# Three edits to the mixers and the first attention: GpSimd's long operations on VectorE, selection rows on 128 rows, logits made kind by kind

## The chip, the cores and the metric

The kernel runs on one core of a Trainium2 chip. The metric is the device time of one execution in microseconds (us). PE is TensorE, which multiplies matrices; DVE is VectorE, ACT is ScalarE, POOL is GpSimd, and SP is SyncE, whose queue issues the loads of weights. Each engine works through its own queue in order, and waits there on semaphores for the others.

## The reference, cut to what matters

There are 256 tokens of width 1024 and three blocks of layers: a first block with a gated recurrence (HGRN2), a forgetting attention and a hierarchical mixture of experts; then twice a SwiGLU, a mixer of three kinds, and a second SwiGLU. The change touches the attention's logits and the mixers.

```python
def fox_mixer(...):                       # 8 heads of 64; blocks of 128 queries
    logits = einsum('bhtd,bhsd->bhts', qb, k) + (cb[..., :, None] - cum[..., None, :])
    logits = where(mask, logits, NEG_INF)
    p = softmax(logits)
...
def ssd_chunked(x, dt, a, bm, cm):        # 16 heads of 64, run forwards and backwards
    seg = a_cs[:, :, :, None] - a_cs[:, :, None, :]
    decay = exp(where(lower, seg, -inf))
    cb = einsum('bclgn,bcsgn->bclsg', cc, bc)
    y_diag = einsum('bclsg,bclsgr,bcsgrp->bclgrp', cb, decay, xd)
...
def second_block(...):                    # for l in range(2)
    y_ssd = ssd_mixer(...); y_mla = mla_mixer(...); y_conv = conv_mixer(...)
    x = x + concatenate([y_ssd, y_mla, y_conv]) @ w_out[l]
```

## The kernel before, in words

**Products.** Every product with weights is done three times in fp32r (`mm3`, L296 to L299): high part by high part, high by low, low by high. `load` (L257 to L280) brings a tile of weights in by SP's queue as `raw`, ACT casts it to `hi` (L275), and one engine subtracts (`lo` = `raw` − `hi`, L276). `hi` and `lo` have five buffers each, and SP's next load waits for the subtraction that frees its `raw`. The subtraction is DVE's unless the caller names another engine.

**Order.** The phases run one after another: first block, mixture of experts, then for each of two layers SwiGLU, mixer, SwiGLU. A scheduler sets the order in every engine's queue from the order of the program, with loads given priority. PSUM has four banks for running work (`wk`) and four for sums (`acc`).

**The first attention's logits** (L772 to L785). Six units make a bank each: four units of two heads by 256 keys, two of four heads by 128 keys. For each head three matmuls go into its part of the bank: q by k with the 64 rows of a head (L781), a row of cumulative decays chosen by a selection matrix on 128 rows (L782), and the causal mask (L783).

**The mixer.** Three kinds of sequence layer make 28 tiles of 128 columns; each is multiplied by its rows of `w_out` and summed. The convolution's group norm takes its inverse roots as a row tile `cvrow`, spread to columns by `epair` (L1405 to L1437), and gives `yn` and its parts `oh` and `ol`. The state-space layer (SSD) works through pairs of heads i = 0 to 7 (loop L1639 to L1653). `decay(i)` (L1549 to L1571), for each of two directions d, puts a mask (L1554) and differences of cumulative decays (L1558, L1562) into a bank; these come from rows chosen by `esel`, held on 48 partitions. ACT takes the exponential (L1564), DVE adds the two (L1567) and multiplies by `cb` (L1569): this is `m`. `outputs(i)` (L1573 to L1606) spreads a row by `epair` (L1576, 48 rows), multiplies `cb` with `xu` (L1584) and `m` with `xt` (L1589, 64 columns), and DVE makes `v` and `y` (L1591 to L1595). Then come `xh` on ACT and `xl` on DVE (L1598, L1599) and the sum of squares `ssq` (L1605). `project(i)` (L1608 to L1624) multiplies by `w_out`. `project_others` (L1626 to L1636) does so for the attention and the convolution while the scan runs.

**GpSimd's share.** Before the change POOL makes, in each of the two mixers, 16 subtractions L276 of `w_out` (the loads in `project` and `project_others`), four `xu` products (L1534) and four of six sums L1605. It also does the convolutions' tap sums (L1368, L1393) and small roots (L307), which stay.

**DVE's chain.** The latent attention's output norm puts a chain of some 15 small operations on DVE: L1840, L305, then Newton's steps of an inverse root in L316 to L321, then L1843. In its queue it lies between `m` of one pair of heads and `y` (L1591, L1593) of the next; `add_to_X` (L331, L333) adds sums to the residual `X`.

Of the kernel before, what the change touches and what calls it, by code (L numbers as in the profile page):

```python
# [11 lines left out]
F32R = mybir.dt.float32r  # L12
# [3 lines left out]
OP = mybir.AluOpType  # L16
# [3 lines left out]
P = 128  # L20
T = 256
# [186 lines left out]
class Kern:  # L208
# [553 lines left out]
    def fox_steps(self, mp, fq, fk, fv, cum, o):  # L762


        nc = self.nc
        e, hd = self.fox_e, self.fox_head
        units = [(1, 0, 0), (1, 1, 0), (1, 0, 2), (1, 1, 2), (0, 0, 0), (0, 1, 0)]
        st = {}

        def heads(u):  # L770
            t, par, j0 = units[u]
            return t, (t + 1) * P, [par + 2 * (j0 + j) for j in range(4 - 2 * t)]  # L772

        def logits(u):
            t, n, hs = heads(u)
            if u == 0:
                st["nh"] = self.split_rows(0, 8, cum[2], -1.0)
            ps = self.bank()
            for j, h in enumerate(hs):
                r = ps[:, j * n:(j + 1) * n]  # L780
                nc.tensor.matmul(r, hd(fq, h)[:, t * P:(t + 1) * P], hd(fk, h)[:, :n], start=True, stop=False)  # L781
                nc.tensor.matmul(r, e(h, P), st["nh"][:, :n], start=False, stop=False)  # L782
                nc.tensor.matmul(r[:, n - P:], self.identb, self.maskb[1], start=False, stop=True)  # L783
            p = st["p", u] = self.t512(mp, "p")
            self.softmax(mp, p, ps, len(hs), 1.0)  # L785

        def turn(u):
            p = st.pop(("p", u))
            ps = self.bank()
            for i in range(4):  # L790
                s = slice(i * P, (i + 1) * P)
                nc.tensor.transpose(ps[:, s], p[:, s], self.ident)
            pt = st["t", u] = self.t512(mp, "pt")
            self.evacuate(pt, ps, u % 2)

        def values(u):
            t, n, hs = heads(u)
            pt = st.pop(("t", u))
            ps = self.bank()
            nb = t + 1  # L800
            for j, h in enumerate(hs):
                for s in range(nb):
                    i = j * nb + s
                    nc.tensor.matmul(ps[:, j * 96:(j + 1) * 96], pt[:, i * P:(i + 1) * P],
                                     fv[:, s, h * 65:h * 65 + 96], start=s == 0, stop=s == nb - 1)
            pair = o[:, t].rearrange("p (a two) d -> p a two d", two=2)
            _, par, j0 = units[u]
            self.normalise_heads(mp, pair[:, j0:j0 + len(hs), par], ps, len(hs))

        return logits, turn, values  # L810


# [390 lines left out]
    def mix_tables(self):  # L1203

        nc = self.nc
        c = self.ctx.enter_context(self.tc.tile_pool(name="late", bufs=1))
        self.epair = c.tile([48, 16, 64], F32R, name="epair")
        nc.vector.tensor_copy(self.epair, self.cfs("esel")[:48].unsqueeze(2).to_broadcast([48, 16, 64]))
        self.rows48 += [self.zero_row(c, i) for i in range(1, 5)]
        posi = c.tile([P, TB], I32, name="posi")  # L1210
        nc.scalar.dma_start(posi, self.io["pos"])
        posf = c.tile([P, TB], F32, name="posf")
        nc.vector.tensor_copy(posf, posi)
        ang = c.tile([P, 2, TB, 16], F32, name="ang")
        kk = c.tile([P, 2, TB, 16], F32, name="angk")
        for t in range(TB):
            nc.vector.tensor_scalar(ang[:, 1, t], self.cfs("inv"), posf[:, t:t + 1], None, op0=OP.mult)
        nc.vector.tensor_scalar(kk[:, 1], ang[:, 1], 1.0 / (2 * math.pi), None, op0=OP.mult)
        nc.vector.tensor_scalar(kk[:, 0], kk[:, 1], 0.25, None, op0=OP.add)
        nc.vector.tensor_copy(ang[:, 0], ang[:, 1])  # L1220
        big = 12582912.0
        nc.vector.tensor_scalar(kk, kk, big, None, op0=OP.add)
        nc.vector.tensor_scalar(kk, kk, -big, None, op0=OP.add)
        c1 = 6.28125
        c2 = float((np.asarray(2 * math.pi - c1, np.float32).view(np.uint32) & np.uint32(0xFFFFF000)).view(np.float32))
        c3 = float(np.float32(2 * math.pi - c1 - c2))
        for cc in (c1, c2, c3):
            nc.vector.scalar_tensor_tensor(ang, kk, -cc, ang, op0=OP.mult, op1=OP.add)
        nc.vector.tensor_scalar(ang[:, 0], ang[:, 0], math.pi / 2, None, op0=OP.add)
        lim = 3.1415925  # L1230
        nc.vector.tensor_scalar(ang, ang, lim, -lim, op0=OP.min, op1=OP.max)
        self.cs = c.tile([P, 2, TB, 32], F32, name="cs")
        for h in range(2):
            nc.scalar.activation(self.cs[:, :, :, 16 * h:16 * h + 16], ang, AF.Sin)
# [169 lines left out]
    def conv_rms(self, mp, cv):  # L1404

        nc = self.nc
        sel = self.cfs("half8").rearrange("p (i a) -> p i a", i=4)
        ps = self.bank()
        for c in range(2):
            sq = self.t512(mp, "cvsq").rearrange("p (a t) -> p a t", a=2)  # L1410
            nc.scalar.activation(sq, cv["y"][:, 2 * c:2 * c + 2], AF.Square)
            for j in range(2):
                i = 2 * c + j
                nc.tensor.matmul(ps[:8, :T], sel[:, i], sq[:, j], start=i == 0, stop=i == 3)
        z = mp.tile([48, T], F32R, name="cvrow", tag="xp0")
        nc.vector.tensor_scalar(z, self.ones[:48].to_broadcast([48, T]), 0.0, None, op0=OP.mult)
        r = mp.tile([8, T], F32, name="cvr", tag="xp1")
        nc.vector.tensor_tensor(r, ps[:8, :T], cv["invb2"][:8], op=OP.mult)
        nc.vector.tensor_scalar(r, r, 1.0 / 64, EPS, op0=OP.mult, op1=OP.add)
        self.newton(r, r, self.t256(mp, "cvr1")[:8], self.t256(mp, "cvr2")[:8])  # L1420
        nc.vector.tensor_tensor(r, r, cv["invb"][:8], op=OP.mult)
        nc.scalar.copy(z[:8], r)
        nc.vector.tensor_tensor(z[32:40], r, z[:8].bitcast(F32), op=OP.subtract)
        cv["row"] = z
# [88 lines left out]
    def ssd_operands(self, mp, S, xs):  # L1513

        nc = self.nc
        u = S["u"]
        xt = mp.tile([P, TB, 16, 64], F32, name="xt", tag="qT")
# [3 lines left out]
        def group(g):  # L1521
            ps = self.bank()
# [6 lines left out]
            for t in range(TB):  # L1529
                ps = self.bank()  # L1530
                for i in range(4):
                    nc.tensor.transpose(ps[:, i * P:(i + 1) * P], xs[:, 4 * g + i, t * P:(t + 1) * P], self.ident)
                nc.scalar.copy(xt[:, t, 8 * g:8 * g + 8].rearrange("p h q -> p (h q)"), ps)
                nc.gpsimd.tensor_tensor(xu[:, t, 8 * g:8 * g + 8], xt[:, t, 8 * g:8 * g + 8],  # L1534
                                        u[:, 16 * t + 8 * g:16 * t + 8 * g + 8].unsqueeze(2).to_broadcast([P, 8, 64]),
                                        op=OP.mult)
        S["xt"], S["xu"], S["cb"] = xt, xu, cb
# [2 lines left out]
    def ssd_scan(self, l, mp, S, xs, zs, wout, mla, cv):  # L1540
# [6 lines left out]
        def decay(i):  # L1547

            ms = []  # L1549
            for d in range(2):  # L1550
# [3 lines left out]
                nc.tensor.matmul(gp, self.identb, self.maskb[d].unsqueeze(1).to_broadcast([P, 4, P]),  # L1554
                                 start=True, stop=False)
                for j in range(2):
                    e = self.esel[:48, 2 * i + j:2 * i + j + 1].to_broadcast([48, P])
                    nc.tensor.matmul(gv[:, j], e, tgt[:48], start=False, stop=False)  # L1558
                e = self.esel[:48, 2 * i:2 * i + 2].unsqueeze(2).to_broadcast([48, 2, P])
                for t in range(TB):  # L1560
                    ts = slice(t * P, (t + 1) * P)
                    nc.tensor.matmul(gv[:, :, ts], src[:48, ts], e, start=False, stop=t == 1)  # L1562
                m = self.t512(mp, f"m{d}")
                nc.scalar.activation(m, gp, AF.Exp)  # L1564
                ms.append(m)
# [7 lines left out]
        def outputs(i, mv):  # L1573
            g = i // 4
            vp = self.bank()
            nc.tensor.matmul(vp[:, :T], self.epair[:, 2 * i:2 * i + 2].rearrange("p a q -> p (a q)"), S["tx"][:48],  # L1576
                             start=True, stop=True)
            v = self.t256(mp, "v")
            nc.scalar.activation(v, vp[:, :T], AF.Exp)
# [20 lines left out]
            if i % 4 == 0:  # L1600
                nc.scalar.activation(ssq[:, g], y, AF.Square)
            else:
                sq = self.t256(mp, "sq")
                nc.scalar.activation(sq, y, AF.Square)
                (nc.vector if i % 4 == 3 else nc.gpsimd).tensor_tensor(ssq[:, g], sq, ssq[:, g], op=OP.add)  # L1605
            return hh, hl  # L1606

        def project(i, hh, hl):  # L1608
# [1 line left out]
            if i % 4 == 0:  # L1610
                S["acc"] = [[self.bank("acc") for _ in range(2)] for _ in range(TB)]
            if i % 2 == 0:
                S["wt"] = self.load(wout[2 + i // 2], eng=nc.gpsimd)
            if i % 4 < 3:
                self.out_tile(S["acc"], S["wt"], i % 2, hh, hl, i % 4 == 0, False)
                return
# [7 lines left out]
                          lambda n, t: self.add_to_X(t, n, S["acc"][t][n], inv[:, g, t:t + 1]))  # L1624

        def project_others(c, ops, n, tag):  # L1626
            wt = self.load(wout[c + n], eng=nc.gpsimd)
            for t in range(TB):
                ps = self.bank(tag)
                if c and n == 1 and t == 1:  # L1630
# [282 lines left out]
```

## Time and profile before

| | us |
|---|---|
| median of 3 runs (lowest to highest) | 1656.97 (1656.61 to 1661.03) |
| the profiled execution | 1659.93 |
| its span on the engines | 1658.1 |
| PE busy | 1605.6 (97%) |
| DVE busy | 1031.5 (62%) |
| ACT busy | 747.2 (45%) |
| POOL busy | 166.3 (10%) |

In the chain that ended last PE holds 62% and DVE 9% of the span. A share over the whole span says little here, since the stages differ. The two scans of the state-space layer lie at about 754 to 840 us and 1374 to 1460 us, the first attention at about 65 to 110 us, and the mixture of experts from about 148 to 410 us. A row of the timeline has the start, the time of the group, engine, line, what is written and read, and partitions x columns; in brackets stands the engine's idle time before it and what ended that.

### The profile page before, as it was taken

The page shows a single profiled execution, that of the slowest core. Times are in us where ns is not written, and L with a number is a line of the kernel's source. Part 1 is how long each engine was busy: PE and PEld are TensorE (multiplying, and loading weights), DVE is VectorE, ACT ScalarE, POOL GpSimd, SP SyncE. Part 2 cuts the span into 40 slices and gives each one's busy share as a digit, 9 for nine tenths or more (in the row PEclk, how much of TensorE's full clock was granted, in tenths as well). Part 3 has the DMA queues.
Part 4 walks back from the last instruction along what each step waited for, and adds up shares of the span by engine and source line. Part 5 has one row for each costly group of instructions (what it writes and reads, how often), then busy time and mean ns, then how long its engine had stood idle before and what let it go on. Part 6 is the DMA issues. An engine that isn't in the chain of part 4 may idle for free.

```text
span 1658.1 us, 25503 instructions
## 1 busy us (share of the span) xinstructions
PE 1605.6 (97%) x10407; PEld 1344.7 (81%) x10407; DVE 1031.5 (62%) x1645; ACT 747.2 (45%) x1219; POOL 166.3 (10%) x145
## 2 busy tenths in 40 slices
PE   8999899997999999998999999999999998999999
PEld 7987444433999989996789998999989996799998
DVE  6967221112756579887765566656569887766564
ACT  5544111111644467554464444444467554454443
POOL 0320000000000002115400000000001115400000
PEclk9999999999999999999999999999999998999999
DMA  9323899998755234432245555455544432245552
GB/s 381 136 77 133 330 415 417 417 417 352 288 187 187 72 136 165 153 106 99 76 153 204 178 182 187 165 180 191 174 167 153 153 120 84 77 156 200 178 193 87
DMA packets 50958, 320.37 MB, mean 193 GB/s; under 512 B 5904, under 2 KB 6160, under 8 KB 17680
## 3 DMA queue, kind: packets, MB, share of 16 engines
q1 hardware_dynamic: 50256, 318.04, 51.9%
q8 instruction: 84, 1.38, 0.3%
q10 hardware_dynamic: 576, 0.60, 0.1%
q14 instruction: 42, 0.34, 0.1%
HBM read 317.58 MB, written 1.05 MB: 192 GB/s over the span
## 4 chain that ended last, share of the span: by engine, by line
PE 62%; DVE 9%; ACT 2%; issue 2%; POOL 0%; ACTq 0%; DVEq 0%
PE wk L297 10%; PE wk L298 10%; PE wk L299 10%; PE acc L297 9%; PE acc L299 9%; PE acc L298 9%; DVE lo L276 2%; DVE xs L1370 1%; ACT hi L275 1%; PE wk L1793 1%; PE wk L1774 1%; DVE ol L1436 1%; PE wk L1558 0%; DVE m L1567 0%; DVE q L1741 0%
## 5 line engine op out<-in xcount | busy, mean ns | idle before, releaser
L276 DVE TENSOR_TENSOR lo<-raw,hi 128x1024 fp32r<-128x1024 f32 (+2 forms) x312 | 378.4, 1224 | 203.1 <-ACT hi L275 199.0
L275 ACT CAST hi<-raw 128x1024 fp32r<-128x1024 f32 (+1 forms) x344 | 354.7, 1042 | 329.3 <-PE wk L298 125.6
L297 PE MATMUL wk<-xh,hi 128*128 128x256 f32 x1344 | 380.7, 283 | 0.0
L299 PE MATMUL wk<-xh,lo 128*128 128x256 f32 x1344 | 380.1, 283 | 0.0
L298 PE MATMUL wk<-xl,hi 128*128 128x256 f32 x1344 | 380.0, 283 | 0.0
L298 PEld LDWEIGHTS wk<-xl,hi 128*128 128x128 f32 x1344 | 257.5, 192 | 1.9
L297 PEld LDWEIGHTS wk<-xh,hi 128*128 128x128 f32 x1344 | 257.5, 192 | 1.7
L299 PEld LDWEIGHTS wk<-xh,lo 128*128 128x128 f32 x1344 | 257.6, 192 | 0.0
L297 PE MATMUL acc<-xh,hi 128*128 128x256 f32 x688 | 199.5, 291 | 0.2
L299 PE MATMUL acc<-xh,lo 128*128 128x256 f32 x688 | 194.7, 283 | 1.8 <-DVE lo L276 1.8
L298 PE MATMUL acc<-xl,hi 128*128 128x256 f32 x688 | 194.7, 283 | 0.5 <-DVE xl L372 0.5
L297 PE MATMUL acc<-hi,hh 128*128 128x512 f32 x352 | 139.5, 397 | 0.4 <-ACT hh L447 0.3
L298 PE MATMUL acc<-lo,hh 128*128 128x512 f32 x352 | 138.6, 395 | 0.0
L299 PE MATMUL acc<-hi,hl 128*128 128x512 f32 x352 | 137.4, 396 | 0.0
L297 PEld LDWEIGHTS acc<-xh,hi 128*128 128x128 f32 x688 | 131.0, 191 | 3.1 <-issue 1.3
L299 PEld LDWEIGHTS acc<-xh,lo 128*128 128x128 f32 x688 | 131.4, 191 | 2.4 <-DVE lo L276 2.2
L298 PEld LDWEIGHTS acc<-xl,hi 128*128 128x128 f32 x688 | 131.6, 191 | 1.9 <-DVE xl L372 0.9
L276 DVE TENSOR_TENSOR lo<-more,hi 128x1024 fp32r<-128x1024 f32 x64 | 81.1, 1276 | 33.2 <-ACT hi L275 32.8
L275 ACT CAST hi<-more 128x1024 fp32r<-128x1024 f32 x64 | 66.0, 1044 | 48.1 <-PE wk L298 18.4
L436 DVE TENSOR_TENSOR gu<-wk,invb 128x512 f32<-128x512 f32 x84 | 58.0, 691 | 47.3 <-PE wk L299 47.2
L276 POOL TENSOR_TENSOR lo<-raw,hi 128x1024 fp32r<-128x1024 f32 x32 | 76.6, 2398 | 94.2 <-ACT hi L275 94.2
L447 ACT CAST hh<-h 128x256 fp32r<-128x256 f32 x88 | 35.7, 406 | 101.9 <-DVE h L444 101.8
(450 smaller groups left out, 2564.7 us busy)
## 6 DMA issues: line engine op xcount, KB each, us to landing
raw<-in_ffn_dram SPq DMA_DIRECT2D x112, 1024.0 KB, 4.7
more<-in_wmoe_dram SPq DMA_DIRECT2D x39, 1024.0 KB, 15.0
raw<-in_win_dram SPq DMA_DIRECT2D x37, 1024.0 KB, 4.8
whole<-in_wmoe_dram SPq DMA_DIRECT2D x66, 512.0 KB, 12.6
raw<-in_wmoe_dram SPq DMA_DIRECT2D x24, 1024.0 KB, 12.7
more<-in_ffn_dram SPq DMA_DIRECT2D x20, 1024.0 KB, 4.8
raw<-in_wout_dram SPq DMA_DIRECT2D x17, 1024.0 KB, 4.9
more<-in_win_dram SPq DMA_DIRECT2D x7, 1024.0 KB, 13.6
```

Source lines behind the costliest of these rows:

```text
L275: nc.scalar.copy(hi[:, :sub], raw[:, s])
L276: (eng or nc.vector).tensor_tensor(lo[:, :sub], raw[:, s], hi[:, :sub].bitcast(F32), op=OP.subtract)
L297: nc.tensor.matmul(out, ah, bh, start=start, stop=False)
L298: nc.tensor.matmul(out, ah, bl, start=False, stop=False)
L299: nc.tensor.matmul(out, al, bh, start=False, stop=stop)
L436: nc.vector.tensor_tensor(gu, gate.rearrange("p (a t) -> p a t", a=2), invb.unsqueeze(1).to_broadcast([P, 2, T]), op=OP.mult)
L447: nc.scalar.copy(hh, h)
L1370: nc.vector.scalar_tensor_tensor(o, xp[:, j, q:q + T], cwh[:, 12 * q + i:12 * q + i + 1], o, op0=OP.mult, op1=OP.add)
L1436: nc.vector.tensor_sub(hl, yn, hh.bitcast(F32))
L1774: nc.tensor.matmul(ps[:, j * T:(j + 1) * T], qT[:, h + j, t * P:(t + 1) * P], kT[:, h + j], start=True, stop=True)
L1793: nc.tensor.matmul(ps[:, j * 96:(j + 1) * 96], pt[:, i * P:(i + 1) * P], v[:, s, (h + j) * 65:(h + j) * 65 + 96], start=s == 0, stop=s == 1)
```

## The change

1. Logits: per unit, first all L782 (128 rows), then one mask matmul over all heads of the unit in place of one each, then all q by k (64 rows).
2. `epair` and `cvrow` grow from 48 to 128 partitions, and L1558, L1562, L1576 read 128 rows in place of 48; the added rows hold zeros.
3. The subtractions for `w_out`, the products `xu` and all sums `ssq` are DVE's: 16 + 4 + 4 operations in each mixer.

```diff
-            for j, h in enumerate(hs):
-                r = ps[:, j * n:(j + 1) * n]
-                nc.tensor.matmul(r, hd(fq, h)[:, t * P:(t + 1) * P], hd(fk, h)[:, :n], start=True, stop=False)
-                nc.tensor.matmul(r, e(h, P), st["nh"][:, :n], start=False, stop=False)
-                nc.tensor.matmul(r[:, n - P:], self.identb, self.maskb[1], start=False, stop=True)
+            rs = [ps[:, j * n:(j + 1) * n] for j in range(len(hs))]
+            m = len(hs)
+            for r, h in zip(rs, hs):
+                nc.tensor.matmul(r, e(h, P), st["nh"][:, :n], start=r is rs[0], stop=False)
+            nc.tensor.matmul(ps.rearrange("p (j n) -> p j n", j=m)[:, :, n - P:], self.identb,
+                             self.maskb[1].unsqueeze(1).to_broadcast([P, m, P]), start=False, stop=False)
+            for r, h in zip(rs, hs):
+                nc.tensor.matmul(r, hd(fq, h)[:, t * P:(t + 1) * P], hd(fk, h)[:, :n], start=False, stop=r is rs[-1])
...
-        self.epair = c.tile([48, 16, 64], F32R, name="epair")
+        self.epair = c.tile([P, 16, 64], F32R, name="epair")
...
-        z = mp.tile([48, T], F32R, name="cvrow", tag="xp0")
+        z = mp.tile([P, T], F32R, name="cvrow", tag="xp0")
...
-                nc.gpsimd.tensor_tensor(xu[:, t, 8 * g:8 * g + 8], xt[:, t, 8 * g:8 * g + 8],
+                nc.vector.tensor_tensor(xu[:, t, 8 * g:8 * g + 8], xt[:, t, 8 * g:8 * g + 8],
...
-                    e = self.esel[:48, 2 * i + j:2 * i + j + 1].to_broadcast([48, P])
-                    nc.tensor.matmul(gv[:, j], e, tgt[:48], start=False, stop=False)
-                e = self.esel[:48, 2 * i:2 * i + 2].unsqueeze(2).to_broadcast([48, 2, P])
+                    e = self.esel[:, 2 * i + j:2 * i + j + 1].to_broadcast([P, P])
+                    nc.tensor.matmul(gv[:, j], e, tgt, start=False, stop=False)
+                e = self.esel[:, 2 * i:2 * i + 2].unsqueeze(2).to_broadcast([P, 2, P])
...
-                    nc.tensor.matmul(gv[:, :, ts], src[:48, ts], e, start=False, stop=t == 1)
+                    nc.tensor.matmul(gv[:, :, ts], src[:, ts], e, start=False, stop=t == 1)
...
-            nc.tensor.matmul(vp[:, :T], self.epair[:, 2 * i:2 * i + 2].rearrange("p a q -> p (a q)"), S["tx"][:48],
+            nc.tensor.matmul(vp[:, :T], self.epair[:, 2 * i:2 * i + 2].rearrange("p a q -> p (a q)"), S["tx"],
...
-                (nc.vector if i % 4 == 3 else nc.gpsimd).tensor_tensor(ssq[:, g], sq, ssq[:, g], op=OP.add)
+                nc.vector.tensor_tensor(ssq[:, g], sq, ssq[:, g], op=OP.add)
...
-                S["wt"] = self.load(wout[2 + i // 2], eng=nc.gpsimd)
+                S["wt"] = self.load(wout[2 + i // 2])
...
-            wt = self.load(wout[c + n], eng=nc.gpsimd)
+            wt = self.load(wout[c + n])
```

The new kernel's lines behind L781 have numbers three higher: L786 is q by k, and L1561 stands where L1558 stood.

Order on PE, at the logits of one unit of two heads (`fq` and `fk` are q and k, `rows` the decays, `mask_excl` the mask, `C` belongs to the recurrence beside it):

```order
-L781 MATMUL wk<-fk,fq 128x256
-L782 MATMUL wk<-rows_228,esel 128x256
+L782 MATMUL wk<-rows_228,esel 128x256 x2
 L783 LDWEIGHTS identb
-L783 MATMUL wk<-mask_excl,identb 128x128
-L781 MATMUL wk<-fk,fq 128x256
-L782 MATMUL wk<-rows_228,esel 128x256
-L783 LDWEIGHTS identb
-L783 MATMUL wk<-mask_excl,identb 128x128
+L783 MATMUL wk<-mask_excl,identb 128x2x128
+L786 MATMUL wk<-fk,fq 128x256 x2
 L713 MATMUL wk<-C 128x128 x8
```

The two 64-row products now stand together, behind the rows and one mask matmul. The sizes in such rows are those of what is written, not the rows that are multiplied.

Order on DVE before, from the latent attention's norm (`oss`, `rsv`, `rsc`, `oinv`) to the first `y` behind it:

```order
L1840 TENSOR_REDUCE oss<-osq 128x8
L331 TENSOR_TENSOR X_73<-acc,X_73 128x512
L305 TENSOR_SCALAR rsv<-oss 128x16
L316 TENSOR_SCALAR rsc<-rsv 128x16
L317 TENSOR_SCALAR rsy<-rsc 128x16
...
L331 TENSOR_TENSOR X_74<-acc,X_74 128x512
L321 SCALAR_TENSOR_TENSOR oinv<-rsc,rsy 128x16
L1843 TENSOR_TENSOR o<-o,oinv 128x512 x2
L1591 TENSOR_TENSOR v<-wk,v 128x256
L1593 SCALAR_TENSOR_TENSOR y<-xs,colt,wk 128x256
```

The same place in the changed kernel:

```order
L305 TENSOR_SCALAR rsv<-oss 128x16
L316 TENSOR_SCALAR rsc<-rsv 128x16
L317 TENSOR_SCALAR rsy<-rsc 128x16
L319 TENSOR_TENSOR rsc<-rsy 128x16
L320 SCALAR_TENSOR_TENSOR rsc<-rsc,rsv 128x16
L276 TENSOR_TENSOR lo<-raw,hi 128x1024
L331 TENSOR_TENSOR X_74<-acc,X_74 128x512
L276 TENSOR_TENSOR lo<-raw,hi 128x1024
L321 SCALAR_TENSOR_TENSOR rsy<-rsc,rsy 128x16
L1594 TENSOR_TENSOR v<-wk,v 128x256
L319 TENSOR_TENSOR rsc<-rsy 128x16
L1596 SCALAR_TENSOR_TENSOR y<-xs,colt,wk 128x256
```

Two subtractions come into the chain, and `v` and `y` (L1594, L1596) no longer stand behind its end, but between its second round of steps.

Order on POOL before, in the first mixer's scan:

```order
L276 TENSOR_TENSOR lo<-raw,hi 128x1024 x3
L1534 TENSOR_TENSOR xu<-xt,u 128x512 x2
L276 TENSOR_TENSOR lo<-raw,hi 128x1024
L1534 TENSOR_TENSOR xu<-xt,u 128x512 x2
L276 TENSOR_TENSOR lo<-raw,hi 128x1024 x6
L1605 TENSOR_TENSOR ssq<-sq,ssq 128x256
...
L307 TENSOR_TENSOR ginv<-rsv,nhalf 128x2
```

In the changed kernel POOL's queue has only the two L307 in this stretch; the rest stands in DVE's.

## Rows read from the trace of the kernel before

**Rows 1.** Windows: length; busy of PE, PEld, DVE, ACT, POOL (count); clock; DMA share; GB/s.
```profile
160.00:410.00 250.00, 236.02 (x1089) 103.07 (x1088) 52.25 (x131) 38.10 (x70) 0.69 (x1) 0.97 0.97 391
735.00:754.00 19.00, 19.00 (x147) 17.27 (x147) 13.37 (x27) 8.79 (x20) 10.31 (x6) 1.00 0.34 112
754.00:840.00 86.00, 78.08 (x388) 57.88 (x389) 68.00 (x107) 38.93 (x70) 37.67 (x21) 0.92 0.28 96
1374.00:1460.00 86.00, 79.57 (x384) 58.83 (x384) 67.43 (x106) 38.76 (x69) 37.83 (x21) 0.90 0.27 93
```

**Rows 2.** Timeline of PE at one unit of the logits, 68.8 to 73 us.
```profile
68.87 0.70 PE L781 MATMUL wk<-fk,fq 64*128 64x256 f32 x2
...
69.89 0.70 PE L781 MATMUL wk<-fk,fq 64*128 64x256 f32 x2
...
70.81 2.00 PE L713 MATMUL wk<-C 128*128 128x128 f32 x16
72.56 0.36 PE L297 MATMUL acc<-xh,hi 128*128 128x256 f32 x1
72.77 0.28 PE L298 MATMUL acc<-xl,hi 128*128 128x256 f32 x1
72.89 0.28 PE L299 MATMUL acc<-xh,lo 128*128 128x256 f32 x1
```

**Rows 3.** Timeline of PE at the first scan's second `decay`, 764.6 to 767.1 us.
```profile
764.60 0.39 PE L299 MATMUL acc<-hi,ol 128*128 128x512 f32 x1
764.83 0.39 PE L1554 MATMUL wk<-mask_low,identb 128*128 128x512 bf16 x1
765.15 0.50 PE L1558 MATMUL wk<-rows,esel 48*128 48x256 f32 x2
...
766.77 0.50 PE L297 MATMUL acc<-hi,oh 128*128 128x512 f32 x1
767.10 0.39 PE L298 MATMUL acc<-lo,oh 128*128 128x512 f32 x1
```

**Rows 4.** Waits of PE, 754 to 840 us: total, times, longest.
```profile
PE wk L1554 <- DVE y L1593: 4.1, 1, 4.1
```

**Rows 5.** Windows of the five spells at half clock; columns as in rows 1.
```profile
779.72:789.96 10.24, 8.34 (x24) 6.16 (x24) 7.47 (x16) 2.40 (x5) 0.00 (x0) 0.50 0.01 2
...
sum 30.71, PE 27.95 PEld 20.87 DVE 21.38 ACT 5.98 POOL 5.41; mean PE 5.59 PEld 4.17 DVE 4.28 ACT 1.20 POOL 1.08
```

**Rows 6.** Groups by line, DVE, 754 to 840 us: count, busy us, mean ns, idle before.
```profile
L1599 DVE SCALAR_TENSOR_TENSOR xl<-y,colt,xh 128x256 fp32r<-128x256 f32 x8 | 9.0, 1124 | 3.7 <-ACT xh L1598 3.7
L1567 DVE TENSOR_TENSOR m<-m,m 128x512 f32<-128x512 f32 x8 | 8.9, 1107 | 2.7 <-ACT m L1564 2.7
L1594 DVE TENSOR_TENSOR y<-y,v 128x256 f32<-128x256 f32 x8 | 6.1, 766 | 0.1
...
L1569 DVE TENSOR_TENSOR m<-m,cb 128x512 f32<-128x512 f32 x8 | 5.5, 683 | 0.0
L1436 DVE TENSOR_TENSOR ol<-yn,oh 128x256 fp32r<-128x256 f32 x4 | 5.0, 1262 | 0.0
...
L1862 DVE SCALAR_TENSOR_TENSOR ol<-wk,colt,oh 128x256 fp32r<-128x256 f32 x4 | 1.8, 473 | 0.0
...
L305 DVE TENSOR_SCALAR rsv<-oss 128x16 f32<-128x16 f32 x1 | 0.2, 163 | 0.0
```

**Rows 7.** Timeline of POOL and of DVE at 772 us, in the norm's chain.
```profile
772.45 4.67 POOL L276 TENSOR_TENSOR lo<-raw,hi 128x1024 fp32r<-128x1024 f32 x2 [2.92 <-ACT hi L275]
...
772.59 2.25 DVE L316 TENSOR_SCALAR rsc<-rsv 128x16 int32<-128x16 int32 x1
774.88 2.28 DVE L317 TENSOR_SCALAR rsy<-rsc 128x16 int32<-128x16 int32 x1
```

**Rows 8.** Groups of the page's part 5: the subtraction L276 on DVE and POOL.
```profile
L276 DVE TENSOR_TENSOR lo<-raw,hi 128x1024 fp32r<-128x1024 f32 (+2 forms) x312 | 378.4, 1224 | 203.1 <-ACT hi L275 199.0
...
L276 POOL TENSOR_TENSOR lo<-raw,hi 128x1024 fp32r<-128x1024 f32 x32 | 76.6, 2398 | 94.2 <-ACT hi L275 94.2
```

More of the change, by code (lines that the diff above doesn't have):

```diff
@@ L1206, in mix_tables @@
         c = self.ctx.enter_context(self.tc.tile_pool(name="late", bufs=1))
-        self.epair = c.tile([48, 16, 64], F32R, name="epair")
-        nc.vector.tensor_copy(self.epair, self.cfs("esel")[:48].unsqueeze(2).to_broadcast([48, 16, 64]))
+        self.epair = c.tile([P, 16, 64], F32R, name="epair")
+        nc.vector.tensor_copy(self.epair, self.cfs("esel").unsqueeze(2).to_broadcast([P, 16, 64]))
         self.rows48 += [self.zero_row(c, i) for i in range(1, 5)]
@@ L1414, in conv_rms @@
                 nc.tensor.matmul(ps[:8, :T], sel[:, i], sq[:, j], start=i == 0, stop=i == 3)
-        z = mp.tile([48, T], F32R, name="cvrow", tag="xp0")
-        nc.vector.tensor_scalar(z, self.ones[:48].to_broadcast([48, T]), 0.0, None, op0=OP.mult)
+        z = mp.tile([P, T], F32R, name="cvrow", tag="xp0")
+        nc.vector.tensor_scalar(z, self.ones.to_broadcast([P, T]), 0.0, None, op0=OP.mult)
         r = mp.tile([8, T], F32, name="cvr", tag="xp1")
```

## The prediction

> **What bounds the kernel now.** PE is busy 97% of the span, so I ask stage by stage what ends PE's waits. Busy time by windows comes first [rows 1]. In the two scans PE has 7.9 and 6.4 us without work, and its clock is granted at 0.92 and 0.90 on the mean: here something other than PE decides. From 160 to 410 us the DMA share is 0.97: that stage ends with its transfers. Next I read PE's timeline, to see what a matmul costs beside its neighbours. In the logits and in `decay`, steps take longer than their columns do, though PE counts as busy [rows 2, 3]. The list of waits names the largest stop of the scan: 4.1 us for `y` of L1593 on DVE [rows 4]. The clock stands at half (1.2 in place of 2.4 GHz) in five spells of the two scans; the first begins inside that stop [rows 5]. The groups of DVE show why `y` is late: operations with both operands in SBUF take 0.7 to 1.1 us where like ones take 0.47 or 0.68 [rows 6], and two tiny ones last until POOL has finished [rows 7].
>
> **Logits.** One head takes 69.89 − 68.87 = 1.02 us [rows 2]. Its columns would take less. L713's sixteen records of 128 columns take 72.56 − 70.81 = 1.75 us, 0.11 each, so L781's two records of 256 take 0.44. L782 takes 0.12, as from 72.77 to 72.89. For the mask, half of that: 0.06. That is 0.62, and 0.40 is left for two changes between 64 and 128 rows, 0.20 each. There are 16 heads by blocks, so 32 changes; grouped, each of six units has two, 12 in all: 20 fewer, **−4.0 us**. The mask matmuls keep their columns. Lower bound nothing (if the excess is not the change of rows), upper bound 16 times 0.40, 6.4. This passes through to the end: the expert weights behind it are a stream that starts after the first block and then fills the DMA engines [rows 1], so a stage that starts 4 us earlier ends 4 us earlier.
>
> **Selection rows.** A `decay` of two directions takes 766.77 − 764.83 = 1.94 us [rows 3]. At 0.23 for each mask (764.60 to 764.83) and 0.12 for each of eight matmuls of 256 columns it would be 1.42: excess 0.52. The first product behind it takes 0.33 in place of 0.23, another 0.10, and I allow the same behind L1576. That is 0.72 for each pair of heads, 5.8 for eight, **−11.5 us** for two mixers. The 64-column L1589 keeps its changes. Nothing is paid for the added rows: L1558 with 48 rows goes by its 256 columns like a matmul of 128 rows. Larger copies of zeros into `epair` and `cvrow` have the same columns per partition: nothing. Bounds: 0 and 14.
>
> The Trainium skill has a rule that speaks against this edit: "TensorEngine Tiling (Array Packing)", section Key Properties, says that matmuls in different row tiles run in parallel, so that filling all rows would forgo it. By that, up to half of 72 matmuls at 0.11 in each mixer, an estimate of 8 us for both, would come back, and the sum would be −23. The trace does not agree: all of these matmuls begin at partition 0 and follow each other at full price [rows 3], and the sum keeps 0. The same section says that a change of tiling mode drains TensorE; the excess of rows 2 and 3 agrees, the page gives no price.
>
> **Operations that leave POOL.** In the first scan's window 12 subtractions, two `xu` and four `ssq` come to DVE: 12 × 1.22 [rows 8] + 2 × 0.68 (as L1569) + 4 × 0.47 (as L1862) [rows 6] = 18.0 us. What goes: L1599 8 × (1.12 − 0.47) = 5.2, L1567 8 × (1.11 − 0.68) = 3.4, L1594 8 × (0.77 − 0.47) = 2.4, L1436 4 × (1.26 − 0.47) = 3.2 [rows 6], and the two tiny ones 2.25 + 2.28 − 2 × 0.16 = 4.2 [rows 6, 7]: 18.4 us, since POOL no longer runs beside them. DVE's load stays near 68.0 − 18.4 + 18.0 = 67.6 us, but its order changes: the first `y` stands behind a shorter piece of Newton's chain, and the whole chain no longer carries two stops of over 2 us. `y` was 4.1 late, and about 4.2 of stops plus the second half of the chain, some 2 us of steps and products, leave its path; two subtractions, 2.4 us, enter. The net is about −4, so this stop mostly goes. But the window shrinks too, from 86 to about 72 us, and DVE then has some 4 us to spare in place of 18. I therefore do not let all of PE's idle time vanish: of 7.9 + 6.4 = 14.3 us I keep 7, **−7.3**. Bounds: 0, or even 3 us more idle in each scan, and −14.3.
>
> Ahead of the scan, from 735 to 754 us, DVE is idle 5.6 us [rows 1] and receives four subtractions and two `xu`, 6.3 us: the convolution's last operations come later, **+1.0** for both mixers (bounds 0 and 4). SP's loads wait for the subtractions; an operation half as long frees `raw` no later, so its queue costs nothing, as long as DVE reaches it (the third rival).
>
> **Clock.** In the five spells PE is busy 27.95 us at half clock [rows 5], so half of that, 14.0 us, is lost. The longest follows the 4.1 us stop [rows 4]. If that stop and the one of `ssq` shrink, their spells go; I keep one long spell, 5 us, **−9.0** (bounds +5 and −14).
>
> **Sum.** −4.0 − 11.5 − 7.3 + 1.0 − 9.0 = −30.8 us against the profiled execution of 1659.93: 1629.1. The median of the runs is 3.0 lower, so 1626 in a run like it. The two ends: all idle time and all lost clock gone is −4.0 − 11.5 − 14.3 − 14.0 = −43.8, or 1613; the other end is the first rival's, with less from the logits.
>
> **Rivals.** *Only the changes of rows pay.* DVE, with 67.6 us of work in some 72, becomes the scan's bound: each stop that goes returns behind a subtraction ahead of `m` or `xl`, and the clock falls as before. For it: little slack, and L276 stands inside the chain now. Against it: the long stop came from the stops of over 2 us [rows 7], which cannot be there without POOL's subtractions. Then −4.0 − 11.5 = −15.5: 1641. Chance 0.20.
>
> *The added rows save nothing*, because the excess in `decay` belongs to its own operands and not to the change from 128 to 48 rows; only logits, stops and clock move: −4.0 − 7.3 + 1.0 − 9.0 = −19.3, 1638. For it: L1558 and L1562 are found with 48 rows alone, so no row separates the two. Against it: the same excess stands at 64 rows [rows 2], with other operands. Chance 0.07.
>
> *Slower: DVE inherits the waiting for `hi`.* POOL waits 94.2 us for ACT's casts ahead of 32 subtractions [rows 8], 47 in each mixer; POOL could afford that, but in DVE's queue `m` and `y` stand behind. It decides as soon as DVE reaches a subtraction before its cast by more than DVE's slack: of 47 us, 18 of idle time are there now and some 2 more come free, so about 27 would fall on the path in each mixer, 54 − 31 = +23: 1680. Against it: DVE's own 312 subtractions wait 203.1 us [rows 8], 0.65 each, 10.4 for sixteen, which the slack holds. Chance 0.05.
>
> **How the numbers follow.** About 5 us (0.3%) is what a measurement of this kernel can tell from no change. My forecast has 0.66, with 1613 to 1634 as its own range; the first rival 0.20, the second 0.07, the third 0.05; 0.02 is left for terms that cancel. The range reaches to both middle rivals with an allowance of 3 us: 1613 to 1644. Faster: 0.66 + 0.20 + 0.07 = 0.93; same 0.02; slower 0.05.
>
> **What would show it.** Logits: a unit of two heads with one gap at each side of its 64-row products. Selection rows: `decay` of both directions in about 1.4 us, and the matmul behind it at 0.23. DVE: L1599 near 0.47, L1567 near 0.68, L316 and L317 under 0.3 us. Waits: the one of L1554 on `y` gone or under 1.5 us, and fewer spells at half clock in the two scans. I am wrong if the scans' windows, start to end, shrink by less than 8 us each, if `decay` keeps its 1.94 us, or if PE waits for `m`, `xl` or L276's `lo` by more than 5 us in a scan.

## The result, and the profile after

The changed kernel takes 1622.8 us (median of 4 runs, 1621.14 to 1623.3) against 1656.86 (by now 4 runs): a ratio of 0.9785, 95% interval 0.9771 to 0.9799, or 34.1 us less. Forecast were 1626 and a range of 1613 to 1644. The profiled execution of the changed kernel took 1621.14, 38.8 less than that of before; 4.7 us of this are the place of the two executions among their runs (3.1 above the median before, 1.7 below it after). So terms read from the two profiles are to be compared with 38.8.

The windows of the changed kernel, with the columns of rows 1: the stretch ahead of the first scan, and both scans over the same pieces of the program as the two 86 us windows of rows 1.

```profile
730.00:749.00 19.00, 18.77 (x144) 17.07 (x144) 16.80 (x35) 9.08 (x20) 0.00 (x0) 1.00 0.41 143
...
748.35:817.84 69.49, 68.00 (x388) 54.19 (x387) 62.02 (x123) 38.24 (x70) 1.56 (x2) 1.00 0.32 114
1352.02:1421.28 69.26, 67.61 (x384) 53.80 (x384) 61.43 (x122) 38.03 (x69) 1.56 (x2) 1.00 0.32 112
```

Each scan is 16.5 and 16.7 us shorter. PE's idle time in them fell from 7.9 and 6.4 us [rows 1] to 1.5 and 1.65, the granted clock is 1.00 throughout, and DVE works 62 us of 69.5.

PE's timeline at the logits of the unit of rows 2, and at the `decay` of rows 3:

```profile
69.22 0.39 PE L782 MATMUL wk<-rows,esel 128*128 128x256 f32 x2
69.45 0.28 PE L783 MATMUL wk<-mask_excl,identb 128*128 128x256 bf16 x1
69.67 1.13 PE L786 MATMUL wk<-fk,fq 64*128 64x256 f32 x4
70.72 2.05 PE L713 MATMUL wk<-C 128*128 128x128 f32 x16
```

```profile
756.59 0.39 PE L1557 MATMUL wk<-mask_low,identb 128*128 128x512 bf16 x1
756.63 0.59 PE L1561 MATMUL wk<-rows,esel 128*128 128x256 f32 x2
757.05 0.39 PE L1565 MATMUL wk<-esel,rows 128*128 128x256 f32 x2
757.28 0.39 PE L1557 MATMUL wk<-mask_excl,identb 128*128 128x512 bf16 x1
...
757.96 0.40 PE L297 MATMUL acc<-hi,oh 128*128 128x512 f32 x1
758.20 0.40 PE L298 MATMUL acc<-lo,oh 128*128 128x512 f32 x1
```

A unit of two heads takes 1.50 us (69.22 to 70.72) where it took 1.94 (68.87 to 70.81). A `decay` of both directions takes 1.37 us in place of 1.94, and the product behind it 0.24 in place of 0.33 [rows 3].

The groups of DVE in the first scan of the changed kernel, 749 to 812 us, with the columns of rows 6:

```profile
L1570 DVE TENSOR_TENSOR m<-m,m 128x512 f32<-128x512 f32 x8 | 5.5, 688 | 0.0
...
L1602 DVE SCALAR_TENSOR_TENSOR xl<-y,colt,xh 128x256 fp32r<-128x256 f32 x8 | 3.8, 481 | 0.1
...
L1597 DVE TENSOR_TENSOR y<-y,v 128x256 f32<-128x256 f32 x8 | 3.4, 423 | 0.1
...
L1439 DVE TENSOR_TENSOR ol<-yn,oh 128x256 fp32r<-128x256 f32 x4 | 1.6, 421 | 0.0
...
L317 DVE TENSOR_SCALAR rsy<-rsc 128x16 int32<-128x16 int32 x1 | 0.2, 174 | 0.0
```

Every operation that was long [rows 6, 7] has its short duration now: `m` 1.11 to 0.69 us, `xl` 1.12 to 0.48, the tiny one 2.28 to 0.17. The waits of PE in the same stretch (total, times, longest):

```profile
PE wk L1579 <- ACT m L1567: 0.7, 1, 0.7
PE wk L1557 <- DVE yn L1435: 0.7, 1, 0.7
```

The 4.1 us for `y` [rows 4] are gone.

### The profile page after: what moved, and what is told of

It reads as the page before. It is cut to its first block, busy times and chain, and to the rows that moved or that the text cites. A ratio compares the mean times of both kernels' runs of the same rounds, so it can differ in the third digit from the quotient of the medians.

```text
span 1619.4 us, 25461 instructions
## 1 busy us (share of the span) xinstructions
PE 1577.9 (97%) x10397; PEld 1334.9 (82%) x10397; DVE 1025.3 (63%) x1693; ACT 745.8 (46%) x1219; POOL 73.6 (5%) x97
## 4 chain that ended last, share of the span: by engine, by line
PE 65%; DVE 6%; ACT 3%; issue 1%; POOL 0%; ACTq 0%; DVEq 0%
PE wk L297 11%; PE wk L298 11%; PE wk L299 11%; PE acc L297 9%; PE acc L298 9%; PE acc L299 9%; DVE lo L276 2%; DVE xs L1373 1%; ACT hi L275 1%; PE wk L1796 1%; PE wk L1777 1%; PE wk L1592 1%; PE wk L1587 1%; PE wk L1557 0%; DVE q L1744 0%
## 5 line engine op out<-in xcount | busy, mean ns | idle before, releaser
L276 DVE TENSOR_TENSOR lo<-raw,hi 128x1024 fp32r<-128x1024 f32 (+1 forms) x344 | 417.5, 1224 | 210.6 <-ACT hi L275 206.1
L276 DVE TENSOR_TENSOR lo<-more,hi 128x1024 fp32r<-128x1024 f32 x64 | 81.1, 1276 | 32.6 <-ACT hi L275 32.6
L297 PEld LDWEIGHTS acc<-hi,hh 128*128 128x128 f32 x352 | 66.5, 189 | 16.1 <-ACT hh L447 2.9
```

What stands on the lines that cost most here:

```text
L276: (eng or nc.vector).tensor_tensor(lo[:, :sub], raw[:, s], hi[:, :sub].bitcast(F32), op=OP.subtract)
L297: nc.tensor.matmul(out, ah, bh, start=start, stop=False)
```

## The experiments

Times are medians in us; each ratio is to the kernel before, run on the same chip. A ratio on record differs by up to 0.0008 from the quotient of the two medians.

| kernel | us | before | ratio (95%) |
|---|---|---|---|
| e1, logits alone | 1651.7 | 1659.02 | 0.9964 (0.9951 to 0.9978) |
| e2, selection rows alone | 1655.21 | 1659.02 | 0.9976 (0.9963 to 0.9988) |
| e3, POOL's operations alone | 1637.42 | 1659.02 | 0.9872 (0.9851 to 0.9893) |
| e4, e2 and e3 together | 1627.56 | 1659.02 | 0.9814 (0.9792 to 0.9837) |
| e5, change, subtractions back | 1660.87 | 1659.61 | 1.0012 (1.0001 to 1.0023) |
| e6, change, small ones back | 1623.11 | 1659.61 | 0.9786 (0.9762 to 0.9809) |
| e7, change with 96 rows | 1621.56 | 1659.61 | 0.9777 (0.9753 to 0.9801) |
| e8, change with 64 rows | 1631.8 | 1659.61 | 0.9835 (0.9812 to 0.9858) |
| e9, change, POOL reads beside | 1635.53 | 1658.73 | 0.9858 (0.9835 to 0.9881) |
| e10, change, POOL writes beside | 1622.15 | 1658.73 | 0.9778 (0.9756 to 0.9801) |
| e11, change, taps on DVE too | 1614.83 | 1658.73 | 0.9735 (0.9713 to 0.9757) |
| e12, e5 with the norm later | 1654.22 | 1660.1 | 0.9963 (0.9949 to 0.9978) |

The theory: changes of row groups cost PE some 0.2 us each, and POOL's operations hold DVE up, whose late `y` stops PE and lets the clock fall. The rivals are those of the prediction.

### One part at a time: e1, e2, e3, e4

e1 takes only the hunk of L778 to L785, e2 only those with 128 rows (`epair`, `cvrow`, L1558, L1562, L1576), e3 only those that put POOL's operations on DVE. e4 is e2 and e3 together.

```diff
 # e3, against the kernel before
-                nc.gpsimd.tensor_tensor(xu[:, t, 8 * g:8 * g + 8], xt[:, t, 8 * g:8 * g + 8],
+                nc.vector.tensor_tensor(xu[:, t, 8 * g:8 * g + 8], xt[:, t, 8 * g:8 * g + 8],
-                (nc.vector if i % 4 == 3 else nc.gpsimd).tensor_tensor(ssq[:, g], sq, ssq[:, g], op=OP.add)
+                nc.vector.tensor_tensor(ssq[:, g], sq, ssq[:, g], op=OP.add)
-                S["wt"] = self.load(wout[2 + i // 2], eng=nc.gpsimd)
+                S["wt"] = self.load(wout[2 + i // 2])
-            wt = self.load(wout[c + n], eng=nc.gpsimd)
+            wt = self.load(wout[c + n])
```

> The kernel before with the logits alone grouped by kind. Theory (each change between 64 and 128 rows costs 0.20 us on PE, 20 of them go): the stretch of the logits shrinks by 4 us and all of it reaches the end, 1653 us against about 1657. Rival (the excess belongs to the q by k products themselves): no change of the stretch, 1657.

> The kernel before with the selection rows alone on 128 rows. Theory (0.72 us for each pair of heads): a decay of both directions falls from 1.94 to about 1.4 us; of the 11.5 us for both scans, some is lost again where PE then only waits longer for DVE's y, which is late by POOL's doing: 8 to 11 us faster, 1646 to 1649. Rival (PE waits for DVE anyway): the decay shrinks but the wait for y grows from 4.1 us by as much, 2 to 5 us faster. Rival (the excess does not come from the change of rows): the decay keeps 1.94 us, no change.

> The kernel before with POOL's subtractions, xu and ssq alone moved to DVE. Theory (POOL stops DVE, and DVE's late y stops PE and brings the clock down): DVE's L1599 near 0.47 and L1567 near 0.68 us, the wait for y gone or under 1.5 us, most of the half-clock spells in the scans gone, 13 to 20 us faster: 1637 to 1644. Rival (DVE becomes the bound, only the row changes paid): within 4 us of before.

> The changed kernel with the logits as before: selection rows and POOL's operations together. Theory (parts add up): 4 us above the changed kernel, 1627, and the gain is the sum of the two kernels that have one of the parts. Rival (each part gives the other its gain, or takes it away): the gain differs from that sum by more than 4 us.

The logits alone gave 7.3 us by the medians, 6.0 by the ratio. In the profile their stretch, from the start of the first matmul to the start of the product behind the last (L792 before, L795 in e1), falls from 37.94 to 33.90 us, by the 4.0 forecast, and e4, without them, is 4.8 slower than the change. What is more than that in e1's medians its edit does not explain: in its profile the scans, which it leaves alone, are 2.6 and 3.0 us shorter, with less time at half clock. So scans with such spells differ by as much without an edit of theirs, and a gain of a few us in e2 has to be read with that in mind.

The selection rows alone gave 3.8 us: the first rival of e2 held. Its `decay` did shrink as in the change, but PE then waited longer for what DVE had late anyway (waits of PE before, 754 to 840 us, then in e2, 745 to 850 us):

```profile
PE wk L1620 <- DVE ssq L1605: 1.1, 1, 1.1
```

```profile
PE wk L1554 <- DVE y L1593: 5.2, 1, 5.2
PE wk L1620 <- DVE ssq L1605: 1.8, 1, 1.8
```

The wait for `y` grew from 4.1 [rows 4] to 5.2 us, that for `ssq` behind it from 1.1 to 1.8, and PE's idle time in both scans from 14.3 [rows 1] to 22.1 us (e2, 754.28 to 838.58 and 1374.20 to 1456.06 us).

POOL's operations alone gave 21.6 us, more than the 13 to 20 expected; in e3 PE has these waits left, 745 to 850 us:

```profile
PE wk L1554 <- DVE yn L1432: 0.5, 1, 0.5
PE wk L1576 <- ACT m L1564: 0.2, 1, 0.2
```

and no spell at half clock lies in its scans. Both together (e4) gave 31.5 us, 6 more than 3.8 and 21.6: the rival of e4 held. With DVE in time the selection rows are worth 9.9 us (1637.42 to 1627.56); with DVE late, 3.8. The profiles show the same in the scans alone. These are the sums over both, of e3 (756.64 to 830.63 and 1364.65 to 1438.26 us), then of e4 (756.10 to 825.77 and 1359.71 to 1429.09 us):

```profile
sum 147.60, PE 146.06 PEld 108.20 DVE 123.98 ACT 76.78 POOL 3.06; mean PE 73.03 PEld 54.10 DVE 61.99 ACT 38.39 POOL 1.53
sum 139.05, PE 135.89 PEld 108.12 DVE 123.52 ACT 76.41 POOL 3.12; mean PE 67.95 PEld 54.06 DVE 61.76 ACT 38.20 POOL 1.56
```

The rows take 10.2 us of work off PE, of which 8.6 shorten the scans.

### The rows: e7 and e8

```diff
 # e8, against the change; in e7 96 stands for 64; L1565 and L1579 likewise
-                    e = self.esel[:, 2 * i + j:2 * i + j + 1].to_broadcast([P, P])
-                    nc.tensor.matmul(gv[:, j], e, tgt, start=False, stop=False)
+                    e = self.esel[:64, 2 * i + j:2 * i + j + 1].to_broadcast([64, P])
+                    nc.tensor.matmul(gv[:, j], e, tgt[:64], start=False, stop=False)
```

> The changed kernel with 96 rows in place of 128 in decay and at L1579. Theory (the cost is that of a change of row groups, and 96 rows lie in the same group as 128): as the changed kernel, a decay of both directions 1.4 us. Rival (any other number of rows than the neighbours' 128 costs): 1.9 us, and 9 us slower.

> The changed kernel with 64 rows in place of 128 in decay and at L1579. Theory (change of row groups): a decay of both directions 1.9 us as with 48 rows, 9 us slower than the changed kernel: 1632. Rival (the cost is of the odd number 48, and 64 is as good as 128): as the changed kernel.

The second `decay` on PE's timeline, of e7 first, then of e8:

```profile
757.14 0.39 PE L1557 MATMUL wk<-mask_low,identb 128*128 128x512 bf16 x1
757.18 0.58 PE L1561 MATMUL wk<-rows,esel 96*128 96x256 f32 x2
...
758.51 0.39 PE L297 MATMUL acc<-hi,oh 128*128 128x512 f32 x1
```

```profile
758.85 0.39 PE L1557 MATMUL wk<-mask_low,identb 128*128 128x512 bf16 x1
759.16 0.50 PE L1561 MATMUL wk<-rows,esel 64*128 64x256 f32 x2
...
760.78 0.50 PE L297 MATMUL acc<-hi,oh 128*128 128x512 f32 x1
```

With 96 rows it takes 1.37 us, as with 128; with 64 rows 1.93, as with 48 before. The kernels follow: 1621.56, not to be told from the change, and 1631.8, 9.0 slower than the change and 10.2 slower than e7. What costs is neither an odd number of rows nor having fewer than the neighbours, but a change between matmuls of up to 64 rows and of more than 64, as far as 48, 64, 96 and 128 show it. The rule of the Trainium skill ("TensorEngine Tiling (Array Packing)", Key Properties) that a change of tiling mode drains TensorE agrees, if matmuls of up to 64 rows count as another mode than larger ones, which no run shows by itself. The Trainium skill gives no price there; here it is 9.0 us for the 16 pairs of heads of both mixers, 0.56 us for each.

### What on POOL costs: e5, e6, e9, e10

e5 is the change with `eng=nc.gpsimd` put back at both loads of `wout`; e6 has the two other lines of POOL back.

> The changed kernel with the 32 subtractions L276 of w_out back on POOL; xu and ssq stay on DVE. Theory (a POOL subtraction of 2.4 us holds up DVE's operations with operands in SBUF alone): L1599 and L1567 and the norm's two tiny operations are long again, the wait for y returns, and 15 to 22 us of the gain go: 1638 to 1645. Rival (it is the small operations that mattered, or POOL's wait for hi): under 5 us slower than the changed kernel.

> The changed kernel with the 8 xu and 8 of 12 ssq back on POOL; the subtractions stay on DVE. Theory: POOL runs 8 us per scan in place of some 38, away from the norm's chain, so at most 3 us slower than the changed kernel: 1623 to 1626. Rival (any POOL work beside the scan brings the late y back): over 5 us slower.

The small ones cost nothing (1623.11). The subtractions cost far more than expected: at 1660.87 nothing is left of the whole change. PE's waits in the first scan of e5, 745 to 835 us:

```profile
PE wk L1557 <- DVE y L1596: 5.0, 1, 5.0
PE wk L1557 <- DVE yn L1435: 4.9, 1, 4.9
PE wk L1860 <- ACT m L1567: 2.8, 1, 2.8
PE wk L1623 <- DVE ssq L1608: 1.8, 1, 1.8
```

and three of the groups of DVE in e5, 740 to 832 us:

```profile
L1537 DVE TENSOR_TENSOR xu<-xt,u 128x512 f32<-128x512 f32 x4 | 5.9, 1513 | 0.9 <-ACT xt L1536 0.9
...
L1326 DVE SCALAR_TENSOR_TENSOR zs<-zth,zs 128x512 f32<-128x512 f32 x2 | 3.6, 1780 | 0.0
L317 DVE TENSOR_SCALAR rsy<-rsc 128x16 int32<-128x16 int32 x1 | 2.3, 2271 | 0.0
```

Besides `y`, the convolution's `yn` is late now, by 4.9 us in each mixer: `xu` and `zs`, 0.68 us alone, take 1.5 and 1.8 on the mean beside POOL's subtractions, ahead of the scan, where DVE works 16.8 of 19.0 us even in the change. In both scans together PE is idle for 30.6 us (749.93 to 838.57 and 1372.72 to 1460.61 us) where the change has 3.1, and its work takes 10.3 us longer, with seven spells at half clock: that is the whole 38 us. Since e5 still has the logits and the rows, which alone gave 7.3 and 3.8, to move the small ones and leave the subtractions looks worse than to move nothing; the kernel that would show it, with logits and rows alone, was not run. No wait of PE in the scan names POOL's `lo`.

The queues of e5 are in another order too. To part this from what POOL does beside DVE, e9 and e10 leave every queue but POOL's in the order of the change.

```diff
 # e9, in load, for wout alone; self.idle is 128x256 and nobody reads it
                 (eng or nc.vector).tensor_tensor(lo[:, :sub], raw[:, s], hi[:, :sub].bitcast(F32), op=OP.subtract)
+                if beside:
+                    for q in [hi[:, 256 * k:256 * k + 256].bitcast(F32) for k in range(3)]:
+                        nc.gpsimd.tensor_tensor(self.idle, q, q, op=OP.subtract)
 # e10, in its place
+                    nc.gpsimd.tensor_copy(self.idle[:, :2], hi[:, :2].bitcast(F32))
+                    nc.gpsimd.memset(self.idle, 0.0)
...
```

> The changed kernel with an extra task on POOL for each of the 32 tiles of w_out's weights: as soon as hi is cast, POOL reads pieces of hi three times (3 operations of 128x256, about 2.6 us in all) and writes a result that nobody reads. The queues of PE, DVE, ACT and SP stand in the same order as in the changed kernel. Theory (POOL's operations hold up DVE's while they read SBUF): DVE's L1602, L1570 and the norm's two tiny operations get longer, PE waits for y again, and 10 us or more are lost, up to the 38 us of the kernel with the subtractions on POOL. Rival (that kernel was slow because lo came late from POOL, and because its queues were ordered otherwise): within 3 us of the changed kernel.

> The same with POOL's extra task made of one two-column copy of hi and eight memsets of 128x256 in place of the three that read: POOL is busy at the same places for some 2 us, and nearly always only writes. Theory (what holds DVE up is reading): within 3 us of the changed kernel. Rival (any running POOL operation holds DVE up): as slow as the kernel with the reads.

Groups of DVE in e9, 740 to 822 us, then POOL's, 740 to 820 us:

```profile
L1606 DVE SCALAR_TENSOR_TENSOR xl<-y,colt,xh 128x256 fp32r<-128x256 f32 x8 | 6.1, 757 | 0.0
L1612 DVE TENSOR_TENSOR ssq<-sq,ssq 128x256 f32<-128x256 f32 x6 | 5.0, 830 | 0.0
```

```profile
L280 POOL TENSOR_TENSOR idle<-hi 128x256 f32<-128x256 f32 x43 | 44.2, 1029 | 32.2 <-ACT hi L276 29.7
```

and groups of the same two kinds in e10 with one of the norm's tiny operations, first of DVE, 749 to 812 us, then of POOL, 740 to 820 us:

```profile
L1613 DVE SCALAR_TENSOR_TENSOR xl<-y,colt,xh 128x256 fp32r<-128x256 f32 x8 | 3.8, 479 | 0.1
L1619 DVE TENSOR_TENSOR ssq<-sq,ssq 128x256 f32<-128x256 f32 x6 | 2.5, 419 | 0.0
...
L327 DVE TENSOR_SCALAR rsc<-rsv 128x16 int32<-128x16 int32 x1 | 0.3, 335 | 0.0
```

```profile
L279 POOL COPY idle<-hi 128x2 f32<-128x2 f32 x14 | 12.8, 912 | 17.4 <-ACT hi L276 17.2
L284 POOL MEMSET idle<- 128x256 f32 x15 | 4.7, 312 | 0.9
```

This is the cleanest proof of the case. Reads by POOL whose result nobody waits for cost 12.7 us (1635.53): `xl` goes from 0.48 to 0.76 us, `ssq` from 0.42 to 0.83. POOL's eight memsets and one small copy for each tile, 8 × 0.31 + 0.91 = 3.4 us, cost nothing (1622.15) and leave the durations of DVE's operations with two inputs as they are. Nor is the cause that POOL's reads hold `hi` longer: ACT's casts wait 2.8 us for POOL in e9, but 10.8 in e10 (740 to 822 us), which loses nothing by it. The Trainium skill ("SBUF — State Buffer", Who interferes with whom) has DVE operations with two SBUF inputs contend with a GpSimd operation that reads SBUF, but not with one that only writes; both kernels agree. The Trainium skill ("SBUF — State Buffer", SBUF: two separate sides) has whichever comes second wait for the whole of the first. The trace of e9 agrees: an `ssq` begun at 787.16 us beside a read of 787.03 to 787.71 ends at 787.99, and POOL's reads, 0.61 us at the shortest, often take 1.59.

### The rest of e5: e12

```diff
 # e12, against e5, in the scan's loop
-            if i == 1:
-                self.head_norm(mp, mla["o"], 8, 64)
             if 0 <= i - 1 < 8:
                 ops[i - 1] = outputs(i - 1, mv.pop(i - 1))
+            if i == 2:
+                self.head_norm(mp, mla["o"], 8, 64)
```

> The kernel with the subtractions on POOL (e5), and the latent attention's norm called after the first two outputs instead of ahead of them, so that in DVE's queue v and y of the first two pairs of heads stand ahead of the norm's chain. POOL still makes all subtractions. Theory (of the 38 us that the subtractions on POOL cost, POOL's reads beside DVE are about 13, and most of the rest is that the queues then put the whole norm's chain ahead of y): PE's wait of 5.0 us for y goes, with a spell at half clock, and 10 us or more come back: 1643 to 1650. Rival (the rest is that lo comes late from POOL, or is spread over all of DVE's operations): within 4 us of e5, 1657 to 1664.

It took 1654.22, 6.7 less than e5: between theory and rival. PE's waits in its first scan, 745 to 850 us:

```profile
PE wk L1557 <- DVE yn L1435: 4.8, 1, 4.8
PE acc L297 <- ACT xh L1601: 2.7, 3, 1.6
PE wk L1623 <- DVE ssq L1608: 1.8, 1, 1.8
PE wk L1860 <- DVE o L1846: 1.5, 1, 1.5
```

The wait for `y` is gone, that for `yn` stays, and smaller ones share out the rest. So of e5's 38 us the place of the norm's chain in the queue is some 7, and reads like e9's some 13, if the two add up, which no run shows. The remaining 18 or so are not settled. Two candidates were not parted: POOL's operations of 2.4 us stop DVE for longer at a time than e9's of 1.0, and `lo` itself comes later.

### Beyond the change: e11

```diff
 # e11, against the change
-            nc.gpsimd.tensor_tensor(o, o, tap, op=OP.add)
+            nc.vector.tensor_tensor(o, o, tap, op=OP.add)
-                nc.gpsimd.tensor_tensor(pp[:, 1:T + 1], pp[:, 1:T + 1], cv["invb2"], op=OP.mult)
+                nc.vector.tensor_tensor(pp[:, 1:T + 1], pp[:, 1:T + 1], cv["invb2"], op=OP.mult)
-        nc.gpsimd.tensor_tensor(kv[:, :, 0:64], kv[:, :, 0:64], inv[:, 1].unsqueeze(2).to_broadcast([P, 16, 64]), op=OP.mult)
+        nc.vector.tensor_tensor(kv[:, :, 0:64], kv[:, :, 0:64], inv[:, 1].unsqueeze(2).to_broadcast([P, 16, 64]), op=OP.mult)
```

> The changed kernel with POOL's other long operations of the mixers on DVE too: the tap sums L1371 (24), L1396 (8) and the product L1745 (2). Theory (POOL's work costs where PE waits for DVE, and in these stretches PE is busy 97% and waits little for DVE): within 3 us of the changed kernel. Rival (every POOL operation that is moved pays): 4 us or more faster; the other rival (DVE, at 111 of 130 us there, is now the bound): 4 us or more slower.

The theory missed and the rival held: 1614.83, 8.0 less than the change and the best kernel here. The windows 600 to 750 us of the change, then of e11:

```profile
600.00:750.00 150.00, 145.19 (x1105) 137.94 (x1104) 128.96 (x252) 97.31 (x192) 20.13 (x31) 1.00 0.41 142
```

```profile
600.00:750.00 150.00, 147.54 (x1124) 140.68 (x1123) 133.31 (x276) 99.58 (x195) 2.67 (x14) 1.00 0.40 143
```

DVE does 17 operations more in each mixer and is busy only 4.35 us longer, while PE has more of the window's work done, 1124 matmuls in place of 1105, and is idle for 2.5 us in place of 4.8. What the expectation overlooked is that DVE waited for POOL's results there and was held up beside its reads (two groups of DVE, 600 to 750 us, of the change, then of e11):

```profile
L1373 DVE SCALAR_TENSOR_TENSOR xs<-xp,cwh,xs 128x256 f32<-128x256 f32 x36 | 17.3, 518 | 2.8 <-POOL xs L1371 2.6
...
L1744 DVE TENSOR_TENSOR q<-q,hinv 128x1536 f32<-128x1536 f32 x1 | 3.1, 3078 | 0.0
```

```profile
L1373 DVE SCALAR_TENSOR_TENSOR xs<-xp,cwh,xs 128x256 f32<-128x256 f32 x36 | 15.8, 478 | 0.1
...
L1744 DVE TENSOR_TENSOR q<-q,hinv 128x1536 f32<-128x1536 f32 x1 | 1.7, 1748 | 0.0
```

## Why the prediction was right, step by step

**Logits**, −4.0 forecast: 37.94 to 33.90 us in the profile of the change too, −4.0. The passage to the end held: the experts' weights set out 3.7 us earlier (144.58 in place of 148.24 us).

**Selection rows**, −11.5: the sign and the mechanism held (e7, e8), the size was a little high: of PE's work 10.2 us go by e4 against e3, and the kernels differ by 9.9 there and by 9.0 between e8 and the change. The excess of `decay`, 0.52 forecast, is 0.57, and the 0.10 behind it was right; the allowance for L1576 was not needed. The rule of the Trainium skill ("TensorEngine Tiling (Array Packing)", Key Properties) on tiles that run in parallel, by which the sum would have been −23, is not borne out here, where all tiles begin at partition 0: 96 and 128 rows cost the same as each other and less than 64.

**PE's idle time**, −7.3 with 7 us kept: it fell by 6.4 and 4.8, 11.2 us. The term was mis-sized because DVE's load was: 62.0 us in the same piece of the program, not 67.6, so that 7.5 us were to spare, not 4. The list of held-up operations was nearly complete, 18.4 us where 19.2 went. But 16.4 us came in place of 18.0, since both `xu` now stand ahead of the scan, and the working counted full durations, while the records of successive operations on DVE overlap: they add up to 73.2 us before and 70.5 after, with DVE busy for 68.0 and 62.0.

**Clock**, −9.0 with one long spell kept: all five spells in the scans are gone. They were worth less than the 14.0 of the working: in e3, which loses them too and keeps the rows as they were, PE's work in the two scans takes 146.1 us in place of 157.7 [rows 1], 11.6 less.

**Ahead of the scan**, +1.0: PE waits 0.7 us for `yn` where it waited 0.5; nothing else is seen.

By the profiles the terms are −4.0 − 10.2 − 11.2 − 11.6 = −37.0, against 38.8 measured. The rest lies outside them: from the first matmul behind the start of the experts to the first scan the program takes 605.8 us before, 603.6 in the change and 608.4 in e3, the same matmuls each time. This stretch differs by some us from execution to execution, whatever the mixers' edits. Against the 38.8 of the profiles the forecast's −30.8 is 8.0 short: idle time 3.9, clock 2.6, the 1.0 ahead of the scan that did not come and the 1.8 from outside, less 1.3 for the rows. That it lies within 3.3 of the 34.1 of the medians is partly luck: the two profiled executions are 4.7 us further apart than the medians.

**The rivals.** That only the changes of rows pay is excluded by e3, where POOL's operations alone gave 21.6 us, while the selection rows alone gave 3.8 of their 11.5. That the rows save nothing is excluded by e7 and e8. That DVE inherits the waiting for `hi` did not come: DVE waits 5.1 us for casts in the scan of the change, less than the 10.4 allowed.

**What the prediction didn't have**: that the parts need each other. The rows are worth 10 us only once DVE is in time. The small operations on DVE are worth nothing when the subtractions are there too (e6), and while POOL still subtracts nothing is left of the whole change (e5).

## What to carry to other kernels

An engine at 10% can be what slows one at 62%: where DVE operations with all operands in SBUF take two or three times what like ones take elsewhere in the same trace, look for what GpSimd reads at that moment, and move the long reader first. Put matmuls of up to 64 rows side by side, or pad them with zeros to more than 64, where they stand between full ones. Price a saving on PE only together with the wait that comes next: while another engine is late, a shorter step buys a longer wait.

## What the runs showed of the hardware that was not expected

- 96 rows behave as 128 do, and 64 as 48: 1.37 and 1.93 us for the same columns.
- POOL's memsets beside DVE operations with two inputs are free (`xl` 0.48 us), its reads are not (0.76 us), even of a tile that is no operand of DVE's operation.
- A tiny DVE operation of 128x16 with one input, L316, is held up like those with two: 2.25 us beside a subtraction on POOL [rows 7], 0.17 without. For it a POOL operation that only writes is enough: in e10 this operation (L327 there) and its neighbours, L328 and a float32 one, take 0.33 us, and each ends 0.03 us behind the end of a memset. By the Trainium skill ("SBUF — State Buffer", Who interferes with whom) an operation with one SBUF input contends only in a two-port mode, which it grants to `tensor_scalar`; the rows agree if these had that mode, which no run shows by itself.
